# Delta-rule scan: keys scaled by both decays where they are written, old outputs added by VectorE, lead-in and split places laid anew

## The chip, the cores and the metric

The kernel runs on one core of one Trainium2 chip. The metric is the device time of one execution in microseconds; of several runs the median is given. A profiled execution has its own time, and its span (first to last instruction) is a little shorter than that time.

A core has a matrix engine (TensorE, PE in the profile, with its weight loads as PEld), VectorE (DVE), ScalarE (ACT), GpSimd (POOL) and a queue engine for DMA issues (SyncE, SP). Each takes its instructions in order; semaphores tie them together. PSUM is the memory that PE writes into, in eight banks; here three of them form the ring `pd` (dense products) and five the ring `pz` (all else).

## The reference

Two equal layers, then a final RMSNorm. Each layer normalises x (2048 tokens, 1024 channels), projects it to all branches at once, and adds a merged result to x. Branch A is a gated delta rule with 4 heads of 128 x 128, run forward and backward over time, branch B a convolution module of width 512.

```
q, k, v = split(silu(conv5(proj)))            # heads of 128; q and k L2-normalised
g = -exp(a_log) * softplus(a_lg + dt_bias)    # log decay, per direction and head
beta = sigmoid(b_lg)
o = delta(q, k, v, g[0], beta[0]) + flip(delta(flip of all, g[1], beta[1]))
y_a = (rms(o) * dn_norm_w * silu(z_a)) @ w_dn_out
u = silu(layer_norm(conv31(cf_val * sigmoid(cf_glu)) + b))
y_b = (u * silu(z_b)) @ w_cf_out
x = x + (sigmoid(gate_0) * y_a + sigmoid(gate_1) * y_b) @ w_out
```

The delta rule is computed in chunks. With g the cumulated log decay in a chunk, S the state, and T the inverse of a triangular matrix of the chunk:

```
v_new = T (beta v) - T (beta k exp(g)) S
o     = exp(g) (q S) + (q k' * decay) v_new
S     = exp(g_last) S + (k exp(g_last - g))' v_new
```

## The kernel before, in words

Activations lie transposed (channels on the 128 partitions, tokens along the row). Dense products are made at nearly full float32 precision from operands split in two parts: `split` rounds a tile on ScalarE (line 157) and subtracts on VectorE (line 158), and each product is three matrix instructions of 512 columns (lines 174 to 176). `weight` loads and splits a weight tile in pieces of four.

*Projection stage.* For each of four heads: the projections of k, q and v, a five-tap convolution on VectorE and a SiLU on ScalarE (`conv_tiles`), then the convolution module's projections for a quarter of its width, whose 31 taps run on VectorE (`conformer_conv`, line 728) in small portions between other work. What follows a projection is queued in `post` and advanced one portion after each dense product (`follow`); longer work lies in `back` and is paid out by cost (`pump`). `keys` (lines 580 to 634) belongs to `post`: it turns k into token-major form with four transposes per quarter of the sequence (line 561), sums its squares on ScalarE (line 589), copies the quarter from PSUM (line 591) and stores it to DRAM in `kv_d[chunk, token, 0, head, :]`; then q's squares (line 599), and the grams k'k and k'q (lines 616, 617), copied by ScalarE (line 619). `values` puts v into `kv_d[chunk, token, 1, head, :]`. The scalars of all tokens, among them `kf` = exp(g_last - g), `eg` = exp(g), `neg` and `dl`, are made by `scalars`, the entry of `post` ahead of the first head's keys.

*Scan stage* (`delta`, lines 812 to 1135). Sixteen chunks of 128 tokens, sixteen steps; in each step two lanes run, d = 0 on chunk `step`, d = 1 on chunk 15 - `step`. Each output chunk is so met twice: up to step 7 a lane stores its output to `o_d`, from step 8 on a lane loads what the other lane stored there (`old`, line 967) and adds its own.

`prep(i)` makes what step i needs, in nine portions spread over the steps before it: (1, 2) loads, (3) masks on POOL (line 889), (4) exponentials on ScalarE (line 895), (5) transposes of the 32 x 32 blocks of the inverse (line 899), eight small copies of them, four on VectorE (line 905) and four on ScalarE (line 907), and the products with the decays (lines 909, 911), (6) small matrix products (line 918) and a copy (921), (7) more of them (928, 931) and VectorE copies (933 to 937), (8) line 942 and 943, copied by ScalarE (945), (9) lines 951 to 954, which end the inverse. `lane` has four portions: (1) the load of `old`, the products of keys and queries with the state (lines 971, 974), values corrected by VectorE (line 976), the queries' part scaled by exp(g) into `o1` on ScalarE (line 980); (2) from step 8 on, `old` + `o1` on POOL (line 983); (3) the products with the inverse (line 987) and their copy (989); (4) the products that advance the state (996, 999) and give the output (1005; added to `old` at line 1007 or to `o1` at 1012). `finish` takes a finished pair of chunks through squares (1026), a Newton rsqrt on VectorE, scaling (1044), transposes (1049) and a product (1050), one step later.

`decay_keys` (lines 850 to 854) multiplies the loaded keys of a chunk by `kf` on POOL, 128 x 512 at a time, once per lane and step, a step ahead of their use at line 996.

PE would idle between these small products. So `delta` takes units of three dense matrix instructions from `self.fill` with `pull(n)`: LEAD holds the numbers of units between the first preparations (the lead-in, lines 1066 to 1093), STEP those in a step, TAIL those at the end. `filler` (lines 1137 to 1157) yields the units of the second half of the gate projection, 256 of them, and then those of `early_merge`, the convolution branch's output projection of the first half. In between it loads u (after unit 239) into one half of a tile and splits it, eight pieces after units SPLIT to SPLIT + 7 = 247 to 254. The order of all instructions of PE, ScalarE, VectorE and POOL in the scan is the written order (`bind`); the order of SP's DMA issues, and everything in the projection stage, is laid by the scheduler at build time.

Of the kernel before, what the change touches and what calls it, by code (L numbers as in the profile page):

```python
# [14 lines left out]
P = 128  # L15
L = 2048
HALF = 1024
NB = 512
D = 1024
KD = 8  # L20
H = 4
NCH = 16
# [5 lines left out]
GAP = 0  # L28
SPLIT = 247
LEAD = (8, 10, 6, 6, 6, 4)  # L30
STEP = (6, 5, 5)
# [45 lines left out]
class Trunk:  # L77
# [502 lines left out]
    def keys(self, hd, kt, qt, vs):  # L580
        nc = self.nc
        v_ = nc.vector
# [3 lines left out]
        def k_out(q, ps):  # L586
            ko = self.st("ko")
            for i in range(4):
                nc.scalar.activation(self.junk, ps[:, i * P:(i + 1) * P], AF.Square,
                                     accum_out=ssk[:, 4 * q + i:4 * q + i + 1])  # L590
            nc.scalar.activation(ko, ps, AF.Copy)
# [18 lines left out]
        for c in range(0, NCH, 2):  # L610
            if c == 8:
                yield
            ps = self.pz()
# [198 lines left out]
    def delta(self):  # L812
# [37 lines left out]
        def decay_keys(ins, d):  # L850
            c, _, kv = ins
            k2 = col(self.kf, d, c)
            nc.gpsimd.tensor_tensor(out=kv[:, 0], in0=kv[:, 0], in1=k2[:, :, None].to_broadcast([P, 4, P]),  # L853
                                    op=ALU.mult)

# [6 lines left out]
        def prep(step):  # L862
# [40 lines left out]
            for b in range(4):  # L903
                r = blk(b)
                v_.tensor_copy(wt[r, :, 32 * b:32 * b + 32], dtm[r])
                d, q = (0, 32 * b) if b < 2 else (1, 32 * (b - 2))
                nc.scalar.activation(pp[r, :, q:q + 32], pt[r, d], AF.Copy)
            for d in range(2):
                v_.tensor_tensor(out=ks[d], in0=ks[d], in1=gbs[d], op=ALU.mult)
# [49 lines left out]
        def lane(step, d, g, wt, c, kq, kv):  # L959
            s = hv(st_all[d])  # L960
            x = kv[:, 1]
            neg, dl, eg = col(self.neg, d, c), col(self.dl, d, c), col(self.eg, d, c)
# [5 lines left out]
            if step:  # L968
                pk = hv(self.pz())
                for hd in range(H):  # L970
                    mm(pk[:, hd, :], kq[:, hd, 0, :], s[:, hd, :], start=True, stop=True)  # L971
                pq = hv(self.pz())
                for hd in range(H):
                    mm(pq[:, hd, :], kq[:, hd, 1, :], s[:, hd, :], start=True, stop=True)  # L974
                for hd in range(H):
                    v_.scalar_tensor_tensor(out=x[:, hd], in0=pk[:, hd, :], scalar=neg[:, hd:hd + 1], in1=x[:, hd],
                                            op0=ALU.mult, op1=ALU.add)
                o1 = ro1()
                for hd in range(H):
                    nc.scalar.activation(hv(o1)[:, hd, :], pq[:, hd, :], AF.Copy, scale=eg[:, hd:hd + 1])  # L980
            yield
            if old is not None:
                nc.gpsimd.tensor_tensor(out=old, in0=old, in1=o1, op=ALU.add)
            yield
# [110 lines left out]
        for step in range(NCH):  # L1095
# [6 lines left out]
            for x in lanes:  # L1102
                next(x)
            if nxt:
                for d in range(2):
                    decay_keys(nxt[d], d)
            next(last)
# [29 lines left out]
    def filler(self):  # L1137
        wcf = self.a["w_cf"][self.l]
        u = None
        for n, v in enumerate(self.gates(1)):  # L1140
            yield v
# [13 lines left out]
        self.u0 = u  # L1155
        self.y1 = self.big([P, KD, HALF], F32, "y1")
        yield from self.early_merge(wcf, ahead)

# [224 lines left out]
```

## Time and profile before

| | |
|---|---|
| three runs | 3201.26, 3201.26, 3204.26 us; median 3201.26 |
| profiled execution | 3196.58 us |
| its span | 3194.8 us |
| scan of layer 0, of layer 1 | about 865 to 1285, 2425 to 2850 us of the span |
| DMA | 501.70 MB, mean 157 GB/s |

How to read it: the page names groups of instructions by line, engine, operation and tiles ("pz<-dh,dl" writes pz and reads dh and dl; in the scan tiles are slices of five big ones, `dl` and `dm` and `dh` in the profile, so the line is the better name). A wait "A <- B" is idle time of the engine just before A, put down to what ended it. In the timeline each row has its start, its length, the engine and line, the shapes, the count of merged instructions, and in brackets the idle time before it. An engine with q behind its name issues a DMA. The busy time by stretch has, after the engines, the clock granted to PE as a share of full speed, the busy share of the DMA engines and GB/s.

### The profile page before, as it was taken

Reading aid. Unit: us, or ns where it says so; the run is one execution under the profiler, and the core shown is the slowest. Engines: PE = TensorE matmul, PEld = TensorE weight load, DVE = VectorE, ACT = ScalarE, POOL = GpSimd, SP = SyncE. Lnnn points to the kernel's source line nnn. Section 1 sums busy time; section 2 is a strip of 40 time slices with the busy share of each in tenths; the row PEclk is TensorE's granted clock in tenths of the full one; section 3 lists DMA queues with packets and bytes.
Section 4 is the critical chain, followed back from the end, with each engine's and each line's share of the span. In section 5 each row is a group of like instructions: output and inputs, shape, how many; then the busy total and the mean of one; then the engine's idle time right before and its main releaser. Section 6 shows DMA issues by size and latency. Waiting matters only on the chain. (4 is left out here: it accounts for less than half of the span.)

```text
span 3194.8 us, 51188 instructions
## 1 busy us (share of the span) xinstructions
PE 3085.8 (97%) x19110; PEld 2707.5 (85%) x19110; DVE 2436.9 (76%) x4409; ACT 1384.3 (43%) x3104; POOL 318.2 (10%) x297
## 2 busy tenths in 40 slices
PE   6999999999999999999999999999999999999998
PEld 5788888888889988887888888888887998888786
DVE  7789898987647797745676989898955678967655
ACT  5625252522344466533345242425234446655332
POOL 3000000000122232000000000000002113300000
PEclk9999999999999999999999999999999999999999
DMA  4323232333688787654413141414357777855634
GB/s 141 91 94 94 85 95 85 94 115 132 201 273 259 255 248 229 194 188 133 134 53 102 66 120 60 120 60 123 119 186 263 236 247 250 282 181 193 206 128 149
DMA packets 427545, 501.70 MB, mean 157 GB/s; under 512 B 96224, under 2 KB 260704, under 8 KB 427296
## 3 DMA queue, kind: packets, MB, share of 16 engines
q1 hardware_dynamic: 354544, 388.58, 39.3%
q10 hardware_dynamic: 64688, 80.09, 7.1%
q0 software_dynamic: 8064, 29.76, 2.5%
q8 instruction: 150, 2.46, 0.3%
q14 instruction: 99, 0.81, 0.1%
HBM read 342.74 MB, written 155.58 MB: 156 GB/s over the span
## 5 line engine op out<-in xcount | busy, mean ns | idle before, releaser
L174 PE MATMUL pd<-h,whi 128*128 128x512 f32 x2816 | 1089.6, 387 | 0.0
L176 PE MATMUL pd<-h,wlo 128*128 128x512 f32 x2816 | 1072.5, 381 | 1.5 <-DVE wlo L158 1.5
L175 PE MATMUL pd<-h,whi 128*128 128x512 f32 x2816 | 1072.6, 381 | 0.0
L728 DVE SCALAR_TENSOR_TENSOR cacc<-gp,vec,cacc 128x1009 f32<-128x1009 f32 (+1 forms) x480 | 616.9, 1285 | 37.9 <-ACT cacc L726 34.8
L176 PEld LDWEIGHTS pd<-h,wlo 128*128 128x128 f32 x2816 | 534.8, 190 | 78.9 <-DVE wlo L158 3.1
L174 PEld LDWEIGHTS pd<-h,whi 128*128 128x128 f32 x2816 | 535.6, 190 | 75.6 <-issue 1.4
L175 PEld LDWEIGHTS pd<-h,whi 128*128 128x128 f32 x2816 | 535.3, 190 | 73.6 <-issue 1.9
L157 ACT ACTIVATE whi<-wraw 128x512 fp32r<-128x512 f32 x400 | 242.8, 624 | 474.6 <-PE pd L175 332.3
L158 DVE TENSOR_TENSOR wlo<-wraw,whi 128x512 fp32r<-128x512 f32 x400 | 283.8, 723 | 147.9 <-ACT whi L157 147.5
L553 DVE SCALAR_TENSOR_TENSOR acc<-cin,vec,acc 128x1022 f32<-128x1022 f32 (+1 forms) x192 | 247.0, 1302 | 14.4 <-ACT acc L551 13.2
L176 PE MATMUL pd<-yhi,wlo 128*128 128x512 f32 x512 | 194.7, 380 | 3.3 <-DVE wlo L158 3.3
L174 PE MATMUL pd<-yhi,whi 128*128 128x512 f32 x512 | 194.5, 380 | 0.6 <-ACT whi L157 0.6
L175 PE MATMUL pd<-ylo,whi 128*128 128x512 f32 x512 | 194.0, 379 | 0.0
L808 ACT ACTIVATE go<-pd,vec 128x512 f32<-128x512 f32 x128 | 86.9, 679 | 141.4 <-PE pd L176 124.7
L529 ACT ACTIVATE cin<-pd 128x512 f32<-128x512 f32 x96 | 57.0, 594 | 157.7 <-PE pd L176 157.4
L176 PEld LDWEIGHTS pd<-yhi,wlo 128*128 128x128 f32 x512 | 96.8, 189 | 18.9 <-DVE wlo L158 5.3
L740 ACT ACTIVATE ao<-pd 128x512 f32<-128x512 f32 x64 | 38.3, 598 | 170.0 <-PE pd L176 170.0
L174 PEld LDWEIGHTS pd<-yhi,whi 128*128 128x128 f32 x512 | 96.8, 189 | 14.7 <-ACT whi L157 1.2
L175 PEld LDWEIGHTS pd<-ylo,whi 128*128 128x128 f32 x512 | 96.8, 189 | 13.5
L174 PE MATMUL pd<-uop,whi 128*128 128x512 f32 x256 | 102.1, 399 | 4.9 <-ACT whi L157 4.9
L853 POOL TENSOR_TENSOR dl<-dl,kf 128x512 f32<-128x512 f32 x64 | 74.7, 1176 | 289.4 <-DMA dl<-kv 245.3
L980 ACT ACTIVATE dm<-pz,eg 128x128 f32<-128x128 f32 x240 | 68.0, 371 | 82.0 <-PE pz L974 74.5
(297 smaller groups left out, 4864.7 us busy)
## 6 DMA issues: line engine op xcount, KB each, us to landing
wraw<-w_in SPq DMA_DIRECT2D x240, 256.0 KB, 3.2
gt<-go ACTq DMA_DIRECT2D x128, 256.0 KB, 4.1
dl<-gr SPq DMA_DIRECT2D x128, 256.0 KB, 5.8
dl<-kq SPq DMA_DIRECT2D x64, 512.0 KB, 5.7
dl<-kv SPq DMA_DIRECT2D x64, 512.0 KB, 6.4
wraw<-w_out SPq DMA_DIRECT2D x96, 256.0 KB, 2.8
kq<-acc SPq DMA_DIRECT2D x16, 1024.0 KB, 5.2
gr<-go ACTq DMA_DIRECT2D x64, 256.0 KB, 2.3
```

Of the source, the lines that this page charges most:

```text
L157: self.nc.scalar.activation(hi, src, AF.Copy)
L158: self.nc.vector.tensor_tensor(out=lo, in0=src, in1=hi.bitcast(F32), op=ALU.subtract)
L174: mm(ps, whi[:, k, :], xhi, start=k == 0, stop=False)
L175: mm(ps, whi[:, k, :], xlo, start=False, stop=False)
L176: mm(ps, wlo[:, k, :], xhi, start=False, stop=k == kk - 1)
L529: nc.scalar.activation(cut(t[:, o + b * NB:o + (b + 1) * NB]), sort(ps), AF.Copy)
L553: self.nc.vector.scalar_tensor_tensor(out=out, in0=t[:, k:k + n], scalar=wc(k), in1=out, op0=ALU.mult, op1=ALU.add)
L728: self.nc.vector.scalar_tensor_tensor(out=acc, in0=t[:, k:k + n], scalar=wc(k), in1=acc, op0=ALU.mult, op1=ALU.add)
L740: nc.scalar.activation(cut(o), sort(ps), func)
L808: nc.scalar.activation(cut(o), sort(ps), AF.Identity, bias=self.vec[:, V_GB + j:V_GB + j + 1])
L853: nc.gpsimd.tensor_tensor(out=kv[:, 0], in0=kv[:, 0], in1=k2[:, :, None].to_broadcast([P, 4, P]), op=ALU.mult)
L980: nc.scalar.activation(hv(o1)[:, hd, :], pq[:, hd, :], AF.Copy, scale=eg[:, hd:hd + 1])
```

## The change

Five edits:

1. `keys` writes k twice, scaled by `kf` of direction 0 into slot 0 and of direction 1 into slot 2 of `kv_d`, which has three slots now, with v between them. A lane loads its own two neighbouring slots. The copy from PSUM becomes, per quarter and direction, four ScalarE copies of 128 x 128 with a scale column. `decay_keys` and its calls go.
2. In `lane`, from step 8 on, the queries' part is no more scaled by ScalarE and added by POOL: VectorE multiplies it by `eg` and adds `old` in one instruction per head, in the lane's second portion. Up to step 7 `o1` is made as before.
3. The four copies of line 905 go from VectorE to ScalarE, interleaved with those of line 907.
4. LEAD is (8, 8, 6, 8, 6, 4) and was (8, 10, 6, 6, 6, 4), and in the lead-in the seventh portion of chunk 0 stands ahead of the fifth of chunk 1.
5. u's pieces are split after units 250, 251, 252, 253, 255, 256, 257 and 258. The last three lie in `early_merge`, so `filler` counts over both generators.

```diff
-SPLIT = 247
-LEAD = (8, 10, 6, 6, 6, 4)
+SPLITS = (250, 251, 252, 253, 255, 256, 257, 258)
+LEAD = (8, 8, 6, 8, 6, 4)
...
-        self.kv_d = self.drm.tile([NCH, P, 2, H, P], F32, name=f"kv{l}")
+        self.kv_d = self.drm.tile([NCH, P, 3, H, P], F32, name=f"kv{l}")
...
-            ko = self.st("ko")
             for i in range(4):
                 nc.scalar.activation(self.junk, ps[:, i * P:(i + 1) * P], AF.Square,
                                      accum_out=ssk[:, 4 * q + i:4 * q + i + 1])
-            nc.scalar.activation(ko, ps, AF.Copy)
-            self.astore(self.kv_d[4 * q:4 * q + 4, :, 0, hd, :].rearrange("c p e -> p c e"),
-                       ko.rearrange("p (c e) -> p c e", e=P))
+            for d in range(2):
+                ko = self.st("ko").rearrange("p (c e) -> p c e", e=P)
+                for i in range(4):
+                    j = 64 * d + 4 * (4 * q + i) + hd
+                    nc.scalar.activation(ko[:, i, :], ps[:, i * P:(i + 1) * P], AF.Copy, scale=self.kf[:, j:j + 1])
+                self.astore(self.kv_d[4 * q:4 * q + 4, :, 2 * d, hd, :].rearrange("c p e -> p c e"), ko)
...
-                self.load(kv, self.kv_d[c])
+                self.load(kv, self.kv_d[c][:, d:d + 2])
...
-                v_.tensor_copy(wt[r, :, 32 * b:32 * b + 32], dtm[r])
                 d, q = (0, 32 * b) if b < 2 else (1, 32 * (b - 2))
                 nc.scalar.activation(pp[r, :, q:q + 32], pt[r, d], AF.Copy)
+                nc.scalar.activation(wt[r, :, 32 * b:32 * b + 32], dtm[r], AF.Copy)
...
-            x = kv[:, 1]
+            x, kd = kv[:, 1 - d], kv[:, d]
...
-                o1 = ro1()
+                if old is None:
+                    o1 = ro1()
+                    for hd in range(H):
+                        nc.scalar.activation(hv(o1)[:, hd, :], pq[:, hd, :], AF.Copy, scale=eg[:, hd:hd + 1])
+            yield
+            if old is not None:
                 for hd in range(H):
-                    nc.scalar.activation(hv(o1)[:, hd, :], pq[:, hd, :], AF.Copy, scale=eg[:, hd:hd + 1])
-            yield
-            if old is not None:
-                nc.gpsimd.tensor_tensor(out=old, in0=old, in1=o1, op=ALU.add)
+                    v_.scalar_tensor_tensor(out=hv(old)[:, hd, :], in0=pq[:, hd, :], scalar=eg[:, hd:hd + 1],
+                                            in1=hv(old)[:, hd, :], op0=ALU.mult, op1=ALU.add)
...
-                    mm(hv(pn)[:, hd, :], kv[:, 0, hd], vn[:, hd, :], start=True, stop=True)
+                    mm(hv(pn)[:, hd, :], kd[:, hd], vn[:, hd, :], start=True, stop=True)
...
-        for d in range(2):
-            decay_keys(ins[d], d)
         pull(LEAD[2])
         go(1)
+        go(0)
         go(1)
-        go(0)
...
-            if SPLIT <= n < SPLIT + 8:
-                b, k = divmod(n - SPLIT, 4)
+            if n in SPLITS:
+                b, k = divmod(SPLITS.index(n), 4)
                 self.split(u[:, k, b * NB:(b + 1) * NB], raw(k, b), raw(k, b).bitcast(F32))
```

More of the change, by code (lines that the diff above doesn't have):

```diff
@@ L977, in lane @@
                                             op0=ALU.mult, op1=ALU.add)
-                o1 = ro1()
-                for hd in range(H):
-                    nc.scalar.activation(hv(o1)[:, hd, :], pq[:, hd, :], AF.Copy, scale=eg[:, hd:hd + 1])
+                if old is None:
+                    o1 = ro1()
+                    for hd in range(H):
+                        nc.scalar.activation(hv(o1)[:, hd, :], pq[:, hd, :], AF.Copy, scale=eg[:, hd:hd + 1])
             yield
             if old is not None:
-                nc.gpsimd.tensor_tensor(out=old, in0=old, in1=o1, op=ALU.add)
+                for hd in range(H):
+                    v_.scalar_tensor_tensor(out=hv(old)[:, hd, :], in0=pq[:, hd, :], scalar=eg[:, hd:hd + 1],
+                                            in1=hv(old)[:, hd, :], op0=ALU.mult, op1=ALU.add)
             yield
@@ L1103, in delta @@
                 next(x)
-            if nxt:
-                for d in range(2):
-                    decay_keys(nxt[d], d)
             next(last)
@@ L1138, in filler, with units @@
         wcf = self.a["w_cf"][self.l]
-        u = None
-        for n, v in enumerate(self.gates(1)):
+        u = ahead = None
+        def units():
+            yield from self.gates(1)
+            self.u0 = u
+            self.y1 = self.big([P, KD, HALF], F32, "y1")
+            yield from self.early_merge(wcf, ahead)
+        for n, v in enumerate(units()):
             yield v
@@ L1151, in filler @@
                 ahead = self.weight(wcf[0], 4)
-            if SPLIT <= n < SPLIT + 8:
-                b, k = divmod(n - SPLIT, 4)
+            if n in SPLITS:
+                b, k = divmod(SPLITS.index(n), 4)
                 self.split(u[:, k, b * NB:(b + 1) * NB], raw(k, b), raw(k, b).bitcast(F32))
-        self.u0 = u
-        self.y1 = self.big([P, KD, HALF], F32, "y1")
-        yield from self.early_merge(wcf, ahead)
     def early_merge(self, wcf, ahead):
```

5 lines of the change are left out of this document (removed).

## The prediction

> **What bounds the kernel now.** I read the page first, then who waited for whom on the matrix engine, then the busy time by stretch, then the timeline of three places in the scan.
>
> ```profile
> PE 3085.8 (97%) x19110; PEld 2707.5 (85%) x19110; DVE 2436.9 (76%) x4409; ACT 1384.3 (43%) x3104; POOL 318.2 (10%) x297
> ```
>
> PE is the bound: it sits idle for 3194.8 - 3085.8 = 109 us of the span, and no edit of this change takes a matrix instruction away. So all that can be won is idle PE time (and time at half clock), and all that can be lost is new idle time. The waits of PE over the whole span tell which idle time the change can touch:
>
> ```profile
> PE pz L918 <- DVE dh L999: 11.2, 4, 5.3
> PE pz L942 <- DVE dh L933: 10.6, 2, 5.3
> PE pz L561 <- ACT acc L540: 8.9, 6, 1.6
> ...
> PE pz L918 <- ACT dh L945: 4.9, 6, 1.4
> ```
>
> The columns are us in total, times, longest. Three of the four lie in the scan. The L942 pair is the lead-in, once per layer; two of the L918 waits on L999, near 5 us each, are the step in which u is split. The same places by stretch (columns: us, busy time of PE, PEld, DVE, ACT, POOL, then the granted clock):
>
> ```profile
> 1026.10:1047.90 21.80, 21.80 (x252) 19.93 (x240) 16.04 (x39) 10.05 (x29) 4.64 (x4) 1.00 0.78 253
> 1142.83:1166.13 23.30, 22.79 (x248) 20.88 (x249) 22.57 (x55) 14.59 (x49) 8.86 (x6) 1.00 0.89 267
> 1212.24:1242.29 30.05, 25.52 (x253) 22.87 (x249) 24.72 (x64) 21.11 (x62) 4.63 (x4) 0.89 0.82 264
> 911.80:918.60 6.80, 4.50 (x54) 3.88 (x55) 3.56 (x8) 0.66 (x2) 3.79 (x4) 0.50 0.75 248
> 1232.60:1239.40 6.80, 5.70 (x44) 4.64 (x45) 3.97 (x12) 3.49 (x16) 0.00 (x0) 0.50 0.70 249
> ```
>
> An early step (the first row) has PE busy all its 21.8 us: there nothing can be won. A late step (step 10, the second row) has 0.5 us of PE idle but DVE busy 22.57 of 23.30: DVE has no room. Step 13 (the third) takes 30.05, because of a wait of 4.5 us and because the clock is granted at 0.50 after it (the fifth row), which costs at most half of 5.70, 2.9 us. After the lead-in's wait the clock falls too (the fourth row): at most 2.3 us.
>
> **The lead-in.** The wait of L942 in layer 0:
>
> ```profile
> 907.76 2.44 ACT L895 ACTIVATE dm<-dm,ngc 128x128 f32<-128x128 f32 x8 [2.90 <-DMA dl<-kv]
> ...
> 910.24 1.36 DVE L909 TENSOR_TENSOR dl<-dl,dm 128x512 f32<-128x512 f32 x1 [0.31 <-ACT dm L895]
> 911.52 2.12 DVE L911 TENSOR_TENSOR dl<-dl,dm 128x512 f32<-128x512 f32 x2
> 913.67 0.28 DVE L933 COPY dh<-pz 32x128 f32<-32x128 f32 x1
> ...
> 914.10 0.44 PE L942 MATMUL pz<-dh,dl 64*64 64x64 f32 x2 [5.34 <-DVE dh L933]
> ```
>
> Chunk 0's copies (L933) stand behind chunk 1's products (L909, L911), and these wait for chunk 1's exponentials. The new order puts the copies first, and LEAD moves two units behind them (8+10+6+6 and 8+8+6+8 are both 30 ahead of L942), so L942 finds its operands. But next on PE is L918 of chunk 1, which needs both L909; the second ends at 911.6, and PE gets there about 0.7 us after 908.8, where it now begins to wait: 2 to 2.5 us of the 5.3 stay. The gain is 2.8 per layer, or 5.1 if the half clock goes too. Whether a gap of this size lowers the clock, the trace has once:
>
> ```profile
> 835.01 1.05 PE L200 MATMUL pz<-con,lnt 128*128 128x1 f32 x8 [2.15 <-DVE lnt L766]
> ...
> 836.70:840.10 3.40, 3.40 (x10) 2.68 (x9) 2.21 (x13) 0.00 (x0) 0.00 (x0) 0.50 0.69 227
> ```
>
> A gap of 2.15 us was followed by half clock, so I take 4 of the 2.8 to 5.1: -8 us for two layers. The Trainium skill ("TensorE: Matmul & The Clock Gate", "Why this matters for your kernels") asks only that gaps stay under about 3 us; by that rule the full 5.1 would come, and the sum below would be 2 us lower; the measured gap speaks against it.
>
> **The old outputs on VectorE.** From step 8 the scaling copies on ACT (L980) and the additions on POOL (L983) become eight instructions on DVE, placed directly behind L976 and of its form. Step 10:
>
> ```profile
> 1144.53 0.93 SPq L145 DMA_DIRECT2D dm<-o  x1
> ...
> 1161.40 2.82 SPq L145 DMA_DIRECT2D dl<-gr  x3
> ...
> 1145.41 2.16 DVE L976 SCALAR_TENSOR_TENSOR dl<-pz,neg,dl 128x128 f32<-128x128 f32 x8
> ...
> 1151.10 0.50 DVE L899 STREAM_TRANSPOSE dh<-dh 128x128 f32<-128x128 f32 x2
> 1151.63 1.18 DVE L905 COPY dl<-dh 32x256 f32<-32x256 f32 x4
> ...
> 1151.61 1.27 ACT L989 ACTIVATE dm<-pz 128x512 f32<-128x512 f32 x2
> 1152.78 1.25 ACT L907 ACTIVATE dh<-dh 32x128 f32<-32x128 f32 x4
> ...
> 1159.74 0.39 ACT L945 ACTIVATE dh<-pz 128x256 f32<-128x256 f32 x1 [1.13 <-PE pz L943]
> ...
> 1152.61 1.33 POOL L983 TENSOR_TENSOR dm<-dm,dm 128x512 f32<-128x512 f32 x1 [2.86 <-DMA dm<-o]
> ```
>
> The cost in DVE time is small: 2.16 us come, the four L905 of 1.18 go. The cost is a new wait. The second lane's old output is asked for at 1144.53, since its buffer is free only when the step before has transposed out of it, and has landed at 1152.61. POOL could wait for that; nothing needed its sum before L1007. DVE is at that place 1147.57 + 1.08 = 1148.65, and stands for 3.96 us. Queued behind it are the rsqrt chain and L899, which today begins 1151.10 - 1147.57 = 3.5 us after L976; the same 3.5 us behind the new additions' end, 1152.61 + 1.08, is 1157.2. ACT takes its instructions in written order, so L907 begins over 4 us later than at 1152.78, and with it L1044, L808, L157 and L945, for which L918 waits on PE (it gets the PSUM tile that L945 empties). POOL's masks (L889) no longer stand behind L983 and L853; nobody waits for them in these steps, so that is put at nothing.
>
> The moved L905 copies add to the same chain. Their price on ACT is not in the trace; the nearest rows are
>
> ```profile
> L945 ACT ACTIVATE dh<-pz 128x256 f32<-128x256 f32 x3 | 1.2, 384 | 10.3 <-PE pz L943 10.3
> L921 ACT ACTIVATE dh<-pz 128x128 f32<-128x128 f32 x3 | 0.8, 278 | 0.0
> ```
>
> so 128 columns more cost 0.106 us, and four copies 1.25 + 4 x 0.106 = 1.67 us (between 1.25, as L907, and 2.4, as four L989 halves). L945 had 1.13 us of room, so 0.5 us reach PE in each of steps 9 to 13 even with no DMA late. The ACT time that L980 frees lies ahead of L989, which waits for PE, and wins nothing. In steps 1 to 7 ACT has no L1044 ahead of L945 and is busy 10.05 of 21.80 us: that idle time hides the copies; without it they would cost their 1.67 a step.
>
> The DMA wait, worked out in the same way (POOL's second start, less L976's end and 1.08 for the first lane's addition), is 4.0, 4.0, 4.5 us in steps 10 to 12 of layer 0 and 3.6, 5.0, 3.0 in layer 1; the last of these six is
>
> ```profile
> 2751.05 2.16 DVE L976 SCALAR_TENSOR_TENSOR dl<-pz,neg,dl 128x128 f32<-128x128 f32 x8
> ...
> 2757.34 1.34 POOL L983 TENSOR_TENSOR dm<-dm,dm 128x512 f32<-128x512 f32 x1 [3.35 <-DMA dm<-o]
> ```
>
> Sum 24.1, with 0.5 each 27. Not all of it will come: a stall x of PE at L918 delays the transposes that release the next load, while the loads queued ahead of it (keys, grams; the row at 1161.40) are asked for once L996 and L942 have run, and drain during the stall; the next wait is shorter by about x. With x = w + 0.5 - x half comes: +13.5 (0 to 27). Step 9's load is early: +0.5 per layer, +1.
>
> **u's splits.** Step 13:
>
> ```profile
> 1214.91 2.16 DVE L976 SCALAR_TENSOR_TENSOR dl<-pz,neg,dl 128x128 f32<-128x128 f32 x8
> ...
> 1220.79 3.69 DVE L158 TENSOR_TENSOR uop<-uop 128x512 fp32r<-128x512 f32 x6
> 1224.94 3.34 DVE L905 COPY dl<-dh 32x256 f32<-32x256 f32 x4
> ...
> 1232.53 1.12 DVE L999 SCALAR_TENSOR_TENSOR dh<-dh,dl,pz 128x128 f32<-128x128 f32 x4
> ...
> 1224.47 1.27 POOL L983 TENSOR_TENSOR dm<-dm,dm 128x512 f32<-128x512 f32 x1 [7.58 <-DMA dm<-o]
> ```
>
> L918 waits for L999, which stands behind all eight splits. In the new layout three splits come in the first pull, four in the second, one after L999: L999 is rid of one split (0.6) and of L905 (3.3, stretched by POOL), and gets 2.2 of additions and a wait of 1224.47 - 1218.15 = 6.3 us, some 3.5 after the same feedback. Net about +1.7 and, with less waiting and no stretched L905 in layer 1, about the same: +3 for both (from -14, if both stalls go with their half clock, to +12).
>
> **Keys at their writing.** POOL loses 64 L853. Loads keep their size. ACT gets, per head, 32 scaled copies for four whole ones, and four more DMA issues. Their scale (kf) is computed by an earlier entry of the same queue of work, so no wait is added for it.
>
> ```profile
> L591 ACT ACTIVATE ko<-pz 128x512 f32<-128x512 f32 x32 | 18.9, 590 | 0.0
> ...
> 1120.58 1.14 ACT L980 ACTIVATE dm<-pz,eg 128x128 f32<-128x128 f32 x4 [0.91 <-PE pz L974]
> ...
> 445.00:465.00 20.00, 20.00 (x118) 18.08 (x117) 20.00 (x21) 16.93 (x60) 0.00 (x0) 1.00 0.47 137
> 465.00:485.00 20.00, 20.00 (x118) 18.13 (x117) 17.04 (x45) 7.14 (x10) 3.34 (x5) 1.00 0.65 193
> 490.69 0.60 ACT L713 ACTIVATE glu<-pd 128x512 f32<-128x512 f32 x1 [16.18 <-PE pd L176]
> ```
>
> That is 8 x 1.14 - 4 x 0.59 = 6.8 us of ACT per head beside the issues, inside a stretch where ACT has 3.1 us free of 20. The idle 16 us that end at 490.69 swallow what is left, but until 474.5, where they begin, ACT has only 3.1 + 9.5 - 7.1 = 5.5 us. So 1.3 us, and up to twice that with the issues, can reach PE, through the PSUM tiles that L616 wants while ACT still squares q. Between 0 and 2.6 I take 1, as three pd tiles cover two projections: +8 for eight heads.
>
> **Sum.** -8 + 1 + 13.5 + 3 + 8 = +17.5. The profiled run took 3196.58 (span 3194.8 and 1.8 around it), the median is 3201.26; the difference is put on the median: 3219 us.
>
> **Rivals.** *Faster:* the old loads land in time, and DVE, freed of POOL, ends all four big stalls. For it: L905 took 3.34 beside POOL and 1.18 alone. The Trainium skill ("SBUF — State Buffer", "Who interferes with whom") has the rule: a Vector instruction with two SBUF inputs and a GpSimd one that reads SBUF shut each other out. The price: L942 10.6 and L918 about 10 of 11.2, half clock about 10, less 5 left at L918 in the lead-in and 4 in the heads: some -21, 3180 us. It decides at a landing of 4.1 us (1148.65 - 1144.53), where step 10 shows 8.1. Against it also: in steps 1 to 12 PE's own idle time is near 0.5 us a step, so a freer DVE wins nothing there. Chance 0.36. *No change:* lead-in -8, waits +14.5, half of step 13's stalls gone (-7), heads hidden: 3201 us, 0.14. *Much slower:* each wait passes whole (+27), step 13 +8, heads +16, lead-in -7: 3245 us; it needs the queue of loads not to drain, 0.13. My forecast has 0.37, by itself 3208 to 3230.
>
> **Numbers.** A measurement here can tell 0.2%, 6.4 us. Slower by more: 0.37 + 0.13 = 0.50; within: 0.14; faster: 0.36. The range 3176 to 3241 leaves out the end of the faster case and half of the slowest.
>
> **What would show it.** Right: DVE waits for DMA dm<-o in steps 10 to 13, L918 waits 2 to 4 us for L945 there, steps of 25 to 27 us; no wait at L942, but one at L918 in the lead-in; PE waits at L616 or L561 in the heads. Wrong: second-lane loads landed before L976 ends, or late steps of 23 us and less.

## The result, and the profile after

The changed kernel takes 3239.66 us (median of four runs, 3238.81 to 3244.97), the kernel before 3201.26 beside it: ratio 1.0121, interval 1.0104 to 1.0139. It is slower by 38.4 us. The forecast was slower by 17.5. The profiled execution took 3244.97 us, its span is 3243.2. It lies 5.3 us above its median, that of before 4.7 below its own, so the two traces differ by 48.4 us, and some 10 of these belong to the two executions and not to the change.

Lines moved a little: L914 is the old L918, L941 the old L945, L972 the old L976, L981 the new additions on VectorE, L905 and L907 the old L909 and L911, L895 the old L899, L902 the old L907, L903 the copies of the old L905 (now on ScalarE), L998 the old L999, L678, L680 and L682 the old L676, L678 and L680, L730 and L742 the old L728 and L740, L1175 the old L1177.

The page's first line, after:

```profile
PE 3107.1 (96%) x19110; PEld 2720.5 (84%) x19110; DVE 2356.4 (73%) x4409; ACT 1424.4 (44%) x3322; POOL 194.5 (6%) x201
```

POOL lost 124 us, VectorE 81 us of busy time, and nothing of it was won: PE's idle time went from 109 to 3243.2 - 3107.1 = 136 us, and PE is 21 us busier with the same 19110 instructions, at a mean granted clock of 0.982 where it was 0.989. Who PE waited for:

```profile
PE pz L914 <- ACT dh L941: 18.3, 8, 6.9
PE pd L176 <- DVE wlo L158: 16.4, 7, 5.8
...
PE pd L174 <- ACT ao L742: 12.2, 2, 6.4
...
PE pd L175 <- DVE uop L158: 5.2, 4, 2.5
```

The lead-in's wait (L942, 10.6) is gone and the L918 waits on L999 fell from 11.2 to 5.1. Two of the four lines shown lie mostly or wholly outside the scan, in the projection stage: of the 16.4 (5.9 before), 10.9 are one wait in head 0 of each layer, and so is all of the 12.2 (not there before). By stretch, before:

```profile
128.93:275.04 146.11, 146.11 (x734) 129.26 (x733) 118.14 (x194) 59.99 (x134) 8.26 (x12) 1.00 0.25 78
890.20:943.35 53.15, 47.81 (x511) 41.08 (x510) 22.92 (x53) 25.41 (x61) 11.60 (x9) 0.94 0.83 279
```

and after:

```profile
130.82:294.53 163.71, 151.98 (x735) 132.41 (x734) 121.55 (x194) 62.08 (x159) 8.50 (x12) 0.96 0.24 76
910.59:956.81 46.22, 45.83 (x510) 39.46 (x509) 19.11 (x40) 28.69 (x73) 7.96 (x6) 1.00 0.94 311
1159.65:1183.32 23.67, 22.89 (x253) 20.98 (x249) 17.80 (x59) 14.97 (x51) 3.02 (x2) 1.00 0.89 283
1229.42:1269.22 39.80, 29.05 (x252) 24.51 (x248) 24.70 (x71) 21.04 (x58) 0.00 (x0) 0.80 0.57 182
```

The stretches are head 0 of layer 0 (from its first transpose at L561 to that of head 1), the lead-in, step 10 and step 13. Head 0 lost 17.6 us, the lead-in won 6.9, step 10 is as long as before (23.67 against 23.30), step 13 lost 9.75. The same stretches, both layers together, with those of the experiments (us; starts taken from the traces; "all else" holds head 3 and ends with PE's last instruction, some 9 us before the end of the span):

| kernel | head 0 | heads 1, 2 | lead-in | steps 1-8 | steps 9-12 | step 13 | all else |
|---|---|---|---|---|---|---|---|
| before | 293.3 | 639.7 | 107.0 | 349.9 | 188.8 | 60.8 | 1545.9 |
| after | 327.6 | 638.3 | 92.4 | 357.4 | 187.7 | 79.9 | 1550.8 |
| e1 keys | 327.6 | 638.4 | 105.2 | 350.3 | 185.8 | 59.0 | 1549.9 |
| e2 old outputs, copies | 293.3 | 639.6 | 106.9 | 349.5 | 187.4 | 70.2 | 1550.4 |
| e3 lead-in | 293.3 | 639.5 | 96.3 | 350.2 | 190.7 | 62.5 | 1550.7 |
| e4 splits | 293.3 | 639.5 | 106.2 | 349.8 | 191.5 | 74.4 | 1552.1 |
| e5 keys, gr ahead | 308.4 | 638.3 | 105.1 | 350.2 | 185.8 | 60.0 | 1545.9 |
| e9 | 293.4 | 658.8 | 93.7 | 349.7 | 185.8 | 59.7 | 1558.8 |
| e11 POOL loaded | 293.3 | 639.7 | 108.4 | 353.3 | 226.1 | 69.0 | 1555.8 |
| e13 | 293.4 | 638.3 | 94.8 | 349.5 | 185.9 | 59.7 | 1544.4 |
| e14 after, head 0 mended | 293.4 | 638.8 | 92.5 | 354.4 | 189.1 | 80.0 | 1549.0 |
| e16 e13 and edit 3 | 293.4 | 638.8 | 92.5 | 351.8 | 189.0 | 63.6 | 1552.7 |

The last column moves by several us between kernels whose edits don't touch what it holds (e9 is the exception: its copies also lengthen head 3, which lies there); in a single profile, differences of that size mean nothing, and the verdicts below go by the medians.

**Head 0.** The timeline before, and then after:

```profile
166.66 1.22 DVE L676 TENSOR_TENSOR sol<-gr 128x1024 f32<-128x1024 f32 x1
...
169.41 1.06 ACT L680 ACTIVATE sol<-sol 128x1024 f32<-128x1024 f32 x1 [2.23 <-POOL sol L678]
```

```profile
180.38 1.12 SPq L145 DMA_DIRECT2D br<-bp  x2
181.54 0.59 SPq L145 DMA_DIRECT2D gr<-gs  x1
...
194.11 11.72 DVE L730 SCALAR_TENSOR_TENSOR cacc<-gp,vec,cacc 128x1009 f32<-128x1009 f32 x9
205.75 1.22 DVE L678 TENSOR_TENSOR sol<-gr 128x1024 f32<-128x1024 f32 x1
208.72 1.06 ACT L682 ACTIVATE sol<-sol 128x1024 f32<-128x1024 f32 x1 [16.64 <-POOL sol L680]
...
211.09 1.08 ACT L742 ACTIVATE ao<-pd 128x512 f32<-128x512 f32 x2
...
211.74 0.79 PE L174 MATMUL pd<-h,whi 128*128 128x512 f32 x1 [6.40 <-ACT ao L742]
...
249.75 1.29 DVE L158 TENSOR_TENSOR wlo<-wraw,whi 128x512 fp32r<-128x512 f32 x2
...
250.50 0.79 PE L176 MATMUL pd<-h,wlo 128*128 128x512 f32 x1 [5.15 <-DVE wlo L158]
```

The order of the instructions no longer fits what the engines do. L678 begins head 0's triangular inverse. In the order laid at build time it now stands behind nine taps (L730) on VectorE, while ScalarE has the inverse's exponential (L682) ahead of the copies that empty PSUM (L742): ScalarE stands 16.64 us, then PE 6.40. Later PE waits 5.15 us for the split of a weight, which VectorE has behind the whole elimination. Two of the loads that L678 needs (gr) are asked for behind loads (br) that wait for a store; before, all four went ahead. After the first of the gaps PE runs at half clock (columns as in the windows above):

```profile
211.70:215.10 3.40, 3.36 (x8) 2.72 (x9) 3.40 (x4) 1.07 (x2) 1.12 (x2) 0.50 0.43 157
```

**Step 10**, after:

```profile
1166.03 1.13 DVE L981 SCALAR_TENSOR_TENSOR dm<-pz,eg,dm 128x128 f32<-128x128 f32 x4 [0.51 <-DMA dm<-o]
...
1160.90 0.89 SPq L145 DMA_DIRECT2D dm<-o  x1
...
1170.05 1.25 DVE L905 TENSOR_TENSOR dl<-dl,dm 128x512 f32<-128x512 f32 x2
1171.22 1.28 DVE L907 TENSOR_TENSOR dl<-dl,dm 128x512 f32<-128x512 f32 x2
```

and before:

```profile
1152.84 3.10 DVE L909 TENSOR_TENSOR dl<-dl,dm 128x512 f32<-128x512 f32 x2
1155.87 3.21 DVE L911 TENSOR_TENSOR dl<-dl,dm 128x512 f32<-128x512 f32 x2
...
1153.90 2.94 POOL L853 TENSOR_TENSOR dl<-dl,kf 128x512 f32<-128x512 f32 x2
1156.81 3.39 POOL L889 TENSOR_TENSOR dm<-dm,con 128x512 f32<-128x512 f32 x2
...
1147.62 0.33 SPq L145 DMA_DIRECT2D dm<-o  x1
```

VectorE waits 0.51 us for the old output, where 3.96 were forecast. And the four products with the decays, which shared their time with POOL, take 2.5 us instead of 6.3. The last row of each view is the request for the second lane's old output: 1.4 us ahead of the start of the first correction after (L972, 1162.33), 2.2 us behind it before (L976, 1145.41). What SyncE's queue stood for longest, before, from 1128 to 1194, is the products with the decays:

```profile
SPq L145 <- DVE dl L911: 22.3, 5, 11.3
```

Behind such a wait, ended at 1133.93, the queue asks for masks, keys and decays, and for the old output of step 10 only at 1147.62, just after one of those loads landed (1147.56). That is 13.7 us after the end of the wait; in the changed kernel, by the same reading, it is 13.3.

**Step 13**, after:

```profile
1238.01 1.13 DVE L981 SCALAR_TENSOR_TENSOR dm<-pz,eg,dm 128x128 f32<-128x128 f32 x4 [2.71 <-DMA dm<-o]
...
1242.21 1.89 DVE L158 TENSOR_TENSOR uop<-uop 128x512 fp32r<-128x512 f32 x3
1244.02 0.50 DVE L895 STREAM_TRANSPOSE dh<-dh 128x128 f32<-128x128 f32 x2
...
1244.36 0.31 ACT L902 ACTIVATE dh<-dh 32x128 f32<-32x128 f32 x1 [4.79 <-DVE dh L895]
...
1255.16 0.63 ACT L1175 ACTIVATE g<-g 128x512 f32<-128x512 f32 x1 [1.91 <-DMA g<-gt]
1255.69 1.13 ACT L157 ACTIVATE uop<-uop 128x512 fp32r<-128x512 f32 x2
1256.73 0.36 ACT L941 ACTIVATE dh<-pz 128x256 f32<-128x256 f32 x1
...
1257.14 0.75 PE L914 MATMUL pz<-dh,dl 32*32 32x32 f32 x32 [6.38 <-ACT dh L941]
```

The wait for the old output comes first, then four splits ahead of the transposes L895, then ScalarE with the first gate (L1175) and two pieces of u ahead of L941. PE waits 2.5 us for a piece of u (the L175 line above) and 6.38 at L914.

### The profile page after: what moved, and what is told of

Its sections match the earlier page's. It is cut to its first block, busy times and chain, and to the rows that moved or that the text cites. A ratio compares the mean times of both kernels' runs of the same rounds, so it can differ in the third digit from the quotient of the medians.

```text
span 3243.2 us, 51220 instructions
## 1 busy us (share of the span) xinstructions
PE 3107.1 (96%) x19110; PEld 2720.5 (84%) x19110; DVE 2356.4 (73%) x4409; ACT 1424.4 (44%) x3322; POOL 194.5 (6%) x201
## 5 line engine op out<-in xcount | busy, mean ns | idle before, releaser
L174 PE MATMUL pd<-h,whi 128*128 128x512 f32 x2816 | 1093.4, 388 | 12.3 <-ACT ao L742 12.2
L176 PE MATMUL pd<-h,wlo 128*128 128x512 f32 x2816 | 1076.1, 382 | 11.0 <-DVE wlo L158 10.9
L175 PE MATMUL pd<-h,whi 128*128 128x512 f32 x2816 | 1077.8, 383 | 0.0
L730 DVE SCALAR_TENSOR_TENSOR cacc<-gp,vec,cacc 128x1009 f32<-128x1009 f32 (+1 forms) x480 | 614.7, 1281 | 35.5 <-ACT cacc L728 31.0
L175 PEld LDWEIGHTS pd<-h,whi 128*128 128x128 f32 x2816 | 537.6, 191 | 73.9 <-issue 1.9
L553 DVE SCALAR_TENSOR_TENSOR acc<-cin,vec,acc 128x1022 f32<-128x1022 f32 (+1 forms) x192 | 246.5, 1299 | 15.0 <-ACT acc L551 13.7
L175 PE MATMUL pd<-ylo,whi 128*128 128x512 f32 x512 | 194.0, 379 | 0.0
L885 POOL TENSOR_TENSOR dm<-dm,con 128x512 f32<-128x512 f32 x64 | 85.5, 1351 | 543.5 <-DMA dm<-gc 520.6
L742 ACT ACTIVATE ao<-pd 128x512 f32<-128x512 f32 x64 | 38.0, 598 | 174.4 <-PE pd L176 170.8
L174 PE MATMUL pd<-uop,whi 128*128 128x512 f32 x256 | 104.7, 409 | 8.3 <-ACT whi L157 5.1
L175 PEld LDWEIGHTS pd<-ylo,whi 128*128 128x128 f32 x512 | 96.8, 189 | 13.6
L175 PE MATMUL pd<-uop,whi 128*128 128x512 f32 x256 | 102.8, 401 | 5.2 <-DVE uop L158 5.2
```

What stands on the lines that cost most here:

```text
L174: mm(ps, whi[:, k, :], xhi, start=k == 0, stop=False)
L175: mm(ps, whi[:, k, :], xlo, start=False, stop=False)
L176: mm(ps, wlo[:, k, :], xhi, start=False, stop=k == kk - 1)
L553: self.nc.vector.scalar_tensor_tensor(out=out, in0=t[:, k:k + n], scalar=wc(k), in1=out, op0=ALU.mult, op1=ALU.add)
L730: self.nc.vector.scalar_tensor_tensor(out=acc, in0=t[:, k:k + n], scalar=wc(k), in1=acc, op0=ALU.mult, op1=ALU.add)
L742: nc.scalar.activation(cut(o), sort(ps), func)
```

## The experiments

**e1: edit 1 alone, in the kernel before.**

> Before, with edit 1 alone (keys scaled at their writing). Theory P (the projection stage's build-time order): in the changed kernel the first head of each layer is 17 us longer than before, by two stalls of PE of 5 to 7 us and the half clock after each, because ScalarE's dense copies stand behind the exponential of head 0's inverse and VectorE's weight split behind its elimination; the other heads keep their 160 us. If edit 1 causes that, this kernel is slower than before by 28 to 38 us, with a stall of L174 on the dense copy and one of L176 on the split in head 0 of both layers. Rival Q (ScalarE's load, as my prediction had it): 1 to 2.6 us in each of eight heads, waits at the grams or transposes, +8 to +20, evenly over the heads. Rival R (any edit lays this order anew): edit 1 alone shifts head 0 by some other amount, and the single edits below shift it too.

Measured 3227.03 us, ratio 1.0076 (1.0064 to 1.0089), +23.8. PE's waits within head 0 of layer 0:

```profile
PE pd L174 <- ACT ao L742: 6.7, 1, 6.7
PE pd L176 <- DVE wlo L158: 5.0, 1, 5.0
```

Head 0 is as long as in the changed kernel, heads 1 and 2 are not longer than before. So theory P holds and rival Q falls. The whole is somewhat less than P's 28, since the lead-in and steps 9 to 13 win 6.6 by the table.

**e2: edits 2 and 3 alone.**

> Before, with edits 2 and 3 alone (old outputs added by VectorE, the four small copies on ScalarE). My prediction: VectorE waits 3 to 5 us for the second lane's load in steps 10 to 12, steps of 25 to 27 us, +14 to +27. Theory S (from the changed kernel's trace, where these waits are 0.5 to 1 us and the late steps last 23.3 as before): -2 to +8, the upper part from steps 1 to 8, which last about 0.3 to 0.6 us longer in the changed kernel. Rival R: head 0 of layer 1 is laid anew and shifts by over 5 us.

Measured 3207.43 us, ratio 1.0015 (1.0006 to 1.0024), +4.2. Step 13 of layer 0, and the wait in it (by stretch, then the timeline):

```profile
1211.42:1245.83 34.41, 27.80 (x253) 24.49 (x249) 24.14 (x68) 21.62 (x61) 4.23 (x4) 0.85 0.65 208
```

```profile
1220.66 1.12 DVE L985 SCALAR_TENSOR_TENSOR dm<-pz,eg,dm 128x128 f32<-128x128 f32 x4 [3.37 <-DMA dm<-o]
```

The late steps lose nothing (step 10 lasts 23.7 us); step 13 loses 9.4 in the two layers, through the wait that was forecast there (6.3 forecast, 3.37 here and 4.55 in layer 1): VectorE splits u behind it, and PE then waits 3.2 and 4.3 us for such a piece. The time lies in theory S's range; steps 1 to 8 are not longer, so that part of S falls. Head 0 is as long as before, and rival R falls.

**e3: edit 4 alone.**

> Before, with edit 4 alone (LEAD and the lead-in's order). Theory of the trace of the changed kernel: the wait at L942 goes and no other takes its place, with the half clock: -5.5 per layer, -9 to -13 in all. My prediction's rival: 2 to 2.5 us come back at L918 of chunk 1, -5 to -8.

Measured 3193.22 us, ratio 0.9964 (0.9950 to 0.9978), -10.0. The lead-in:

```profile
891.24:939.26 48.02, 46.13 (x510) 39.58 (x509) 24.95 (x53) 25.55 (x61) 10.76 (x9) 1.00 0.90 305
```

5.1 us less than before, and the clock is 1.00 where it was 0.94. What came back at L918 is 1.9 us in three waits, the longest 1.2, and the clock stays full through them.

**e4: edit 5 alone.**

> Before, with edit 5 alone (u's pieces split later). Theory T (the later places alone make step 13 late, since three dense products now ask for their piece of u just after it is split, and VectorE's splits stand ahead of the transposes of the inverse): step 13 lasts 38 to 41 us as in the changed kernel, +15 to +20 in all. Rival U (it takes the wait for the old output, 2.7 us in step 13, and ScalarE's four more copies, which this kernel lacks): step 13 lasts 28 to 33 us, -5 to +6.

Measured 3216.99 us, ratio 1.0038 (1.0024 to 1.0052), +13.7. Step 13 lasts 37.0 and 37.4 us: nearer to T than to U. But most of it is not the reason that T gave: PE waits up to 7.9 us for L945, since ScalarE's first gate stands 4.1 us for its load with two pieces of u and L945 behind it, and only then 2.4 us for a piece just split.

**e5: edit 1, its gr loads ahead.** The four gr loads are moved in front of the loop over the matrix:

```
+            for b in range(4):
+                self.load(gr[b:128:4, :], gv[hd][:, b, :])
             for d in range(2):
...
             for b in range(4):
-                self.load(gr[b:128:4, :], gv[hd][:, b, :])
                 self.load(br[b:128:4, :], bv[hd][:, b, :])
```

> Edit 1 alone again, and in head 0 to 3's inverse the four small loads of its decays (gr) asked for ahead of the eight loads of its matrix, instead of between the loads of its scales (br); ScalarE's work stays as edit 1 makes it. Theory P': with edit 1 alone two of the four gr loads stand on SyncE's queue behind the first br loads, which wait for a store; so the build lays the first instruction of the inverse behind nine taps on VectorE, and ScalarE, which has its exponential ahead of the dense copies, waits 16.6 us. With gr ahead, head 0 goes back from 164 to 146 to 150 us: 28 to 36 us less than edit 1 alone, 3190 to 3202 us, at or below before. Rival Q' (ScalarE's longer work in head 0 is the cause, whatever the order): head 0 stays over 158 us, 3215 us or more.

Measured 3207.19 us, ratio 1.0019 (1.0010 to 1.0027): +5.4, where e1 had +23.8. Head 0 is 154 us long: neither the 146 to 150 of P' nor Q''s 158. Its waits:

```profile
PE pd L176 <- DVE wlo L158: 4.7, 1, 4.7
```

The first stall is gone, with ScalarE's work unchanged, so that one was the order of the loads. The second stays, with the split still late on VectorE; what puts it there is not shown.

**e6: the changed kernel, its first gate loaded early** (after unit 247 instead of 256).

> The changed kernel, with the first gate of the early merge loaded ten units earlier, after unit 247 (its buffer is held so much longer). Theory V: in step 13 ScalarE stands 1.9 us for this load (4.1 us with edit 5 alone), with two pieces of u and the copy L941 queued behind it; with the load early the wait goes, and step 13 falls from 40 to 35 to 38 us, -4 to -10 in all. Rival W: what makes L941 late is VectorE's L895 behind four splits and the late old output; the splits on ScalarE then wait for nothing less, and step 13 stays at 39 to 41 us.

Measured 3232.56 us, ratio 1.0106 (1.0092 to 1.0120). Step 13 lasts 39.2 and 37.2 us, the wait at L914 is still 6.1 in both layers, though ScalarE no longer stands for the first gate's load ahead of L941. So the gate's load is not what makes L941 late here, as W said. The time is 7 us below the changed kernel's, as V said, and layer 1's step 13 lies in V's range; but of the profile's difference only 3.4 us lie in step 13, with 2.9 in head 0 and 5.5 in steps 1 to 8, which this edit doesn't touch.

**e7: the changed kernel, u split where it was.**

> The changed kernel, with u split after units 247 to 254 as before. If edit 5's price adds to the others: 3224 to 3230 us, step 13 at 34 to 36 us as with edits 2 and 3 alone. If the steps 1 to 8 (which last 1.2 and 2.3 us longer, and step 8 alone 3.2 and 0.8, in the changed kernel, and in none of the four single edits) belong to the sum of edits 1 to 4 and not to edit 5, they stay longer here too.

Measured 3228.70 us, ratio 1.0086 (1.0073 to 1.0099), 11 less than the changed kernel. Step 13 lasts 34.9 and 34.5. Steps 1 to 8 are still 5 us longer than before: they don't belong to edit 5.

**e8: edits 1 (with gr ahead) and 4.**

> Before, with edit 1, its loads of gr ahead, and edit 4 (the lead-in): without edits 2, 3 and 5. If the parts add: edit 4 gives 10, edit 1 some 2 per layer in the late steps, 3180 to 3190 us, 0.4 to 0.7% faster than before. If the gain of edit 4 depends on POOL's work in the lead-in, which edit 1 takes away, less: 3190 to 3196 us.

Measured 3193.37 us, ratio 0.9974 (0.9965 to 0.9982): no better than edit 4 alone. The lead-in wins 13.3 and steps 9 to 12 win 2.9 by the profile, but head 0 still costs 14.7. The time is that of the second forecast, but its reason is not there: the lead-in wins more than with edit 4 alone (10.7), not less.

**e9: edits 1 and 4, the scaled copies on VectorE.**

```
-                for i in range(4):
-                    j = 64 * d + 4 * (4 * q + i) + hd
-                    nc.scalar.activation(ko[:, i, :], ps[:, i * P:(i + 1) * P], AF.Copy, scale=self.kf[:, j:j + 1])
+                j = 64 * d + 16 * q + hd
+                v_.tensor_tensor(out=ko, in0=ps.rearrange("p (c e) -> p c e", e=P),
+                                 in1=self.kf[:, j:j + 13:4, None].to_broadcast([P, 4, P]), op=ALU.mult)
```

> Before, with edit 1 but its scaled copies on VectorE (one instruction per quarter and direction, eight per head), and edit 4. Theory: ScalarE's longer work in head 0 is what made the build lay the inverse of head 0 late; without it the order of head 0 is that of before, head 0 lasts 146 to 149 us, and edit 4 and a POOL that is free of 64 instructions remain: 3180 to 3190 us. Rival: eight VectorE instructions of 0.7 us per head come in its way instead, and heads last 1 to 2 us longer each, 3190 to 3200 us.

Measured 3208.19 us, ratio 1.0023 (1.0013 to 1.0032). Head 0 is back at 146.2 and 147.2, so ScalarE's copies are what shifts it. But heads 1 and 2 are now 3 to 5.5 us longer each, more than the rival said.

**e10: e9, u split after units 245 to 248 and 256 to 259, first gate early.**

> The same kernel, with u's pieces split after units 245, 246, 247, 248, 256, 257, 258 and 259 (three of them in step 12) and the first gate of the early merge loaded ahead. Theory: the stall of 4.8 us in step 13 is VectorE's time ahead of the state's update, so fewer splits in step 13's first pull bring it down from 30 to 24 to 27 us, -6 to -12 in all against the kernel with label e9_dve. Rival: step 12 has no free time on VectorE and loses what step 13 wins, or PE waits for a piece just split: -3 to +5.

Measured 3218.99 us, ratio 1.0057 (1.0044 to 1.0069). It is 11 us slower than e9: PE waits 2.2 us at the end of step 12, and step 13 lasts 34.7 and 33.6, with a wait of 3.5 and 3.8 us for a piece just split. The rival holds, and the loss is larger than it said.

**e11: e2, and POOL loaded again.** Behind VectorE's additions a line for each lane:

```
+                nc.gpsimd.tensor_tensor(out=ro1(), in0=old, in1=old, op=ALU.add)
```

> Before, with edits 2 and 3, and two additions more on POOL per late step, behind VectorE's additions and ahead of POOL's keys and masks, where POOL's own additions stood before; their results go nowhere. Theory K: in the kernel before, POOL's late additions push its keys and masks onto VectorE's products with the decays (3.1 us for two instead of 1.25); this frees the buffers of the next loads later, and so the old outputs land late, 7 us after the start of VectorE's correction instead of 3.6. With POOL's queue put back, the products are stretched again, the second lane's output lands 2 to 4 us later, VectorE waits 2 to 5 us for it in steps 10 to 12 and those steps last 24 to 27 us: +5 to +20 against edits 2 and 3 alone, as my prediction had it. Rival L: the loads come early for another reason (the four copies gone from VectorE, the order on SyncE's queue): waits of 0.5 to 1.5 us, steps of 23.4 us, within 4 us of edits 2 and 3 alone.

Measured 3253.57 us, ratio 1.0166 (1.0152 to 1.0180), 46 more than e2. Steps 9 to 11 last 28.7 to 30.4 us (step 12 lasts 23.9). But VectorE does not wait for the old output (0.3 to 0.5 us), and the products with the decays are not stretched. What is stretched is the rsqrt of `finish`, on VectorE ahead of the transposes:

```profile
1161.41 1.20 DVE L196 SCALAR_TENSOR_TENSOR orr<-rst,orr 128x8 f32<-128x8 f32 x1
1162.64 1.20 DVE L194 TENSOR_TENSOR rst<-orr,rsv 128x8 f32<-128x8 f32 x1
1163.88 0.17 DVE L195 TENSOR_TENSOR rst<-rst,orr 128x8 f32<-128x8 f32 x1
...
1161.31 2.51 POOL L889 TENSOR_TENSOR dm<-dm,con 128x512 f32<-128x512 f32 x2
```

So neither K nor L holds as written. POOL's place decides, but by what of VectorE it falls on; and since the steps are 6 us longer here, the loads have time enough, so this kernel says nothing on why they landed early in e2.

**e12: the changed kernel, the scaled copies on VectorE.**

> The changed kernel, with the scaled copies of the keys on VectorE. Theory: this takes the price of edit 1 in head 0 away, 17 us in each layer, and nothing else: 3202 to 3210 us, which is what my prediction's sum would have come to without its term for the heads. Rival: head 0 is one of several places that the build lays anew, and the time moves by less than 20 us.

Measured 3237.64 us, ratio 1.0118 (1.0103 to 1.0133). Head 0 won 34 us back and heads 1 and 2 lost 21 of them, as in e9. The time moved by 2 us, as the rival said; the price in head 0 did go, as the theory said.

**e13: edits 1 and 4, head 0's copies alone on VectorE.** The line of e9 for `hd == 0`, those of edit 1 for the other heads.

> Before, with edits 1 and 4, where the scaled copies of head 0 alone are made by VectorE (eight instructions per layer) and those of heads 1 to 3 by ScalarE as in edit 1. Theory: the price of edit 1 lies in head 0's order alone; with it gone head 0 lasts 146 to 147 us and heads 1 to 3 159.3 to 160, and the gains of the lead-in and the late steps are left: 3174 to 3184 us. Rival (every one of the heads pays for the scaled copies, on whichever engine): head 0 or heads 1 to 3 last 3 us longer or more, 3190 us or more.

Measured 3180.40 us, ratio 0.9937 (0.9920 to 0.9953): 20.5 us faster than before, and the fastest of all. Head 0 and head 1 of layer 0; the row below them is head 1 of the kernel before:

```profile
125.85:272.02 146.17, 146.17 (x735) 129.31 (x734) 122.86 (x202) 57.16 (x129) 8.29 (x12) 1.00 0.28 85
272.02:431.91 159.89, 157.99 (x786) 138.95 (x785) 146.53 (x218) 65.37 (x161) 7.58 (x11) 1.00 0.31 96
```

```profile
275.04:435.00 159.96, 158.04 (x786) 138.99 (x785) 146.84 (x218) 61.33 (x134) 8.38 (x11) 1.00 0.28 90
```

PE is busy in all of head 0. In head 1 ScalarE has 4.0 us more to do (its scaled copies take 9.2 us where the whole ones took 2.4) and the head is no longer for it.

**e14: the changed kernel, head 0's copies alone on VectorE.**

> The changed kernel, with the scaled copies of head 0 alone on VectorE. Theory: 17 us per layer come back, and the rest of the changed kernel's time stays where it is (lead-in -7, step 13 +9.5 per layer): 3202 to 3210 us. Rival: the scan's losses depend on what the projection stage did to the order, and step 13 or steps 1 to 8 change by over 3 us.

Measured 3207.42 us, ratio 1.0025 (1.0013 to 1.0037), 32 less than the changed kernel. The theory holds. Step 13 stays at 80.0 for both layers; steps 1 to 8 are 3.0 shorter, at the edge of the rival's 3.

**e16: e13 and edit 3.**

> The kernel with label e13_head0, and edit 3 (the four small copies on ScalarE). My prediction: 0.5 us more at L918 in each late step, +4 to +6 in all. Rival: VectorE, 1.2 us shorter, ends the state's update of step 13 earlier: -1 to -4 in all.

Measured 3187.78 us, ratio 0.9959 (0.9942 to 0.9975), 7.4 more than e13. PE's waits in steps 9 to 13 of layer 0, in e16 and then in e13:

```profile
PE pz L918 <- DVE dh L999: 6.1, 1, 6.1
PE pz L918 <- ACT dh L945: 3.5, 3, 1.3
```

```profile
PE pz L918 <- DVE dh L999: 4.8, 1, 4.8
PE pz L918 <- ACT dh L945: 1.5, 3, 0.5
```

The forecast's 0.5 us a step is there (0.67), the stall of step 13 grew by 1.3 instead of shrinking, and steps 1 to 8 lost another 2.3 in the two layers.

## Why the prediction was wrong

The direction was right and the size was not: +38.4 for +17.5. That 3239.66 still lies inside the stated range (3176 to 3241) is luck: the case at its upper end had other causes. Two terms were far too small (keys, u's splits), one cost that was forecast did not come (old outputs), and steps 1 to 8, put at nothing, cost 7.5 in the profile. Term by term:

- **Keys at their writing**, forecast +8: the step that failed. The sum took the order of the projection stage as given and priced ScalarE's longer work in it. The work was sized rightly (9.2 us for 2.4, 6.8 more) and its price is nil (e13's head 1 is no longer). But this order is laid at build time, as the section on the kernel before says, and with longer work on ScalarE it was laid otherwise: 17.9 and 16.4 us in head 0 of the two layers (e1), taken back in full when head 0's copies leave ScalarE (e13; e14 in the changed kernel, -32). That the keys now need kf is not the cause: e13's copies on VectorE read the same kf and feed the same stores. Of the two stalls, one is the place of the gr loads (e5); why the weight's split went behind the elimination was not tried further. Why the build chose this order is not shown either.
- **Old outputs in steps 9 to 12**, forecast +14.5: measured none (e2). Two readings failed. The first is the row at 1144.53: by the semaphores that POOL's additions wait for, it is the load of the next step's first lane. The second lane's is the one asked for at 1147.62 and landed at 1152.45. So the load takes 4.8 us and not 8.1, and what was late was its request; in the changed kernel it is asked for at 1160.90 and takes 5.0. The faster rival's landing of 4.1 us rests on the same row. The second is the sentence that nobody waits for POOL's masks, "so that is put at nothing". The request follows the products with the decays, for which SyncE's queue waits (step 10 above).

  In before, POOL's keys and masks lie on VectorE's products, which take 6.5 us and end 13.7 us after the step's first correction; with POOL out of the way they take 2.8 and end after 10.2. With edit 1 alone (e1) they end after 12.2 to 13.0, and the loads land 5.9 to 6.9 us after the next correction's start: between before (6.1 to 8.1) and after (2.9 to 4.3). In steps 9 to 11 of all kernels, where those steps last 23 to 25 us, the next step's second old output lands 16.4 to 18.9 us after the end of these products, so it came 3.5 us earlier, and the landing time read from before did not hold. That the products' end sets the request fits all these traces but was not tried by itself, and why the landing ranges over 2.5 us is not shown.

  The Trainium skill ("SBUF — State Buffer", "Who interferes with whom") has the rule, which the forecast used for its faster rival only, and there beside a copy with one input (L905), which that rule does not cover: a VectorE instruction with two inputs in SBUF and a GpSimd one that reads SBUF keep each other out. The trace agrees for the products, which have two: 3.10 us for a pair beside POOL, 1.25 without it.
- **The copies of L905**, 0.5 a step: right in size (e16). With the rest it costs 7.4, of which some 2 in steps 1 to 8, put at nothing there. In e2, with POOL's keys still in place, these steps lost nothing; why they do without them stays open, as do up to 5 us more in steps 1 to 8 of the changed kernel and of e7.
- **u's splits**, forecast +3: 13.7 alone, 19 in step 13 with edit 2. Of the 19, 8.5 stay with the splits in their old place (e7), by the late old output. The forecast counted VectorE only, up to L999. It left out ScalarE, where the pieces of the second pull stand behind the first gate and ahead of L941, and that the product just behind asks for its piece at once. How the 6.4 and 6.9 us at L914 divide between the pieces on ScalarE and its late start behind L895 is not shown; the gate's load adds little (e6).
- **Lead-in**, forecast -8: -10 alone, -14.6 in the changed kernel's profile. The remainder was feared to be one wait of 2 to 2.5 us; it is three of 1.9 in all (e3), and the clock stays full. The one gap of 2.15 us from which the forecast took the half clock was not the only one of its size: those of 2.06 and 2.25 us in the same trace (2394.11, 1454.92) were followed by full pace.

The four single edits add up to -10.0 + 4.2 + 13.7 + 23.8 = +31.7; edit 3's price beside edits 1 and 4 (7.4, e16) is as large as the rest, but that it is the rest is not shown. The "much slower" rival (3245) came near the time by luck: its waits in steps 10 to 12 came nowhere.

## What to carry to other kernels

Where a build lays the order of a stage, lengthening one engine's work there can cost far more than that work: look for the instructions that were laid by the old lengths, and keep the lengths (here by moving one head's copies) before pricing the load. A landing time read from the trace of before is a result of what the change removes as well as of what it keeps; ask what the load's request waited for, and check by the semaphores whose load a row is. When an engine is emptied, look first at what it shared time with.

## What the runs showed of the hardware

In e11 a VectorE instruction of 8 columns, 0.17 us alone, takes 1.20 us beside a POOL instruction and ends with it (1162.64 + 1.20 = 1163.84, where POOL's L889 ends at 1163.82). Five of them are stretched like this, beside five POOL instructions, and 4 us come into a chain of short steps (6.8 us from L1041 to L1044, 2.5 for the same steps in e2). PE's gap of 2.51 us at 1242.95 in the changed kernel was followed by 3.4 us at a granted clock of 0.51, like the 2.15 us of the forecast; gaps of 1.4 to 1.6 us (L561) were followed by the full pace of 0.216 us per dense instruction. Length alone does not decide: a gap of 2.25 us (1454.92, before) was followed by full pace too, and one of 2.32 us (1443.36, e13) by 0.427 us per dense instruction.
